# Two more weight units split ahead of the K/V stage, in a pair buffer that stands empty during the first SwiGLU; the attention's output buffer taken at its first use

## The chip, the core and the metric

The kernel runs on one core of a Trainium2 chip. The metric is device time in microseconds (us), the median over runs. TensorE (PE) multiplies matrices, VectorE (DVE), ScalarE (ACT) and GpSimd (POOL) do the elementwise work, and SyncE (SP) issues almost every DMA.

## The reference, cut to what matters

```python
def short_conv_mixer(h, w_in, conv_w, w_out): ...       # layer 0
def swiglu(h, w_gu, w_down):
    g, u = jnp.split(h @ w_gu, 2, axis=-1)
    return (jax.nn.silu(g) * u) @ w_down
...
for layer in range(DEPTH):                               # two layers
    if layer < N_A_LAYERS:
        h = h + short_conv_mixer(rms_norm(h, a_norm[i]), a_w_in[i], a_conv[i], a_w_out[i])
    else:                                                # K/V from the stream after layer 0
        shared = shared_kv(h, kv_norm, w_kv, ...)        # six K/V sets, two of them compressed
        h = h + nsa_mixer(rms_norm(h, b_norm[i]), b_w_qg[i], b_w_o[i], *shared)
    h = h + swiglu(rms_norm(h, f_norm[layer]), f_w_gu[layer], f_w_down[layer])
return rms_norm(h, final_norm)
```

There are 256 tokens, the model is 1024 wide, a SwiGLU is 2816 wide, and everything is float32.

## The kernel before, in words

**Precision by splitting.** Every float32 operand of a matmul is split in two: `hi` is a rounded copy and `lo` is the rest, `x - hi`. A weight unit is a tile of 128 x 1024 that a DMA loads (`w_...`); ACT writes its hi (`h_...`, line 322), and DVE or POOL writes its lo (`l_...`, line 326). A product is then three matmuls (`mm3`, lines 396 to 398: hi by hi, hi by lo, lo by hi), or two in the first 20 of the 22 pieces of a SwiGLU (lines 658 and 660).

**Stages.** Short convolution (from the start to about 105 us), first SwiGLU (to 289 us), K/V and Q projections with the compression MLP (to about 350 us), attention (to 441 us), second SwiGLU, final norm. Between two stages `residual_tail` adds the last products to `h` (DVE, line 523) in four steps, and the next norm's input is formed chunk by chunk, eight chunks in all: `n` hi on ACT (line 447), `n` lo on DVE (line 451), and the square `n_sq` on ACT (line 456). POOL adds the eight squares one after another (`n_acc`, line 461). PE turns the sum (`n_ss`, line 468), DVE and POOL make the reciprocal root from it (`n_ms`, `n_rtok`), PE spreads it (`n_bc`, line 481), and DVE copies it to `n_rbc`; only the gated part of a SwiGLU needs it, the matmuls start before it is there.

**Streams of weights.** `wa` and `wr` are two streams of units. `ahead(n)` loads and splits units until n are ready. The split parts lie in rings of three buffers (tags `a` and `r`); a ring's buffer comes free when PE has read the unit in it. The raw K/V and output units (`w_kv...`, `w_O...`) have four buffers of their own. The K/V units come in the order in which the plan takes them: K2a, K0a, K0b, K1a, K1b, K2b, Q0a, K4a, Q0b, K4b, then the compression weights Y and the values V.

**Large buffers.** `pair` gives 128 x 2 x 2048 floats from three buffers. The inputs of the norms (`n0`, `n1`, and `n2` twice), the compression's input `xc`, every second `pt` and the attention's output `o_all` take turns in them.

**What sets the order.** The program is written once, in order; a scheduler then places each engine's instructions by a timeline of its own, and each engine runs its list strictly in order. `in_order` (table `ord`) names the engines that keep the written order: from the end of the convolution to the second piece of the first SwiGLU these are PE and POOL alone, so there DVE, ACT and SP stand as the scheduler put them. The K/V and attention stage is written by the table `plan`: H is one chunk of the second n2, K, Q, Y, V are matmuls on a unit, A is one unit more of `wa`.

Of the kernel before, what the change touches and what calls it, by code (L numbers as in the profile page):

```python
# [8 lines left out]
F32 = mybir.dt.float32  # L9
# [7 lines left out]
P = 128  # L17
D = 1024
S = 256
KC = D // P  # L20
FH = 2816
NF = FH // P
# [146 lines left out]
 'qdma': 0,  # L169
 'sq': {'n1': 0, 'n3': 1},  # L170
 'units': {'GP': ('a', False),
           'K0a': ('a', False),
           'K0b': ('a', False),
           'K1a': ('r', False),
           'K1b': ('r', False),
           'K2a': ('a', False),
           'K2b': ('a', False),
           'K4a': ('a', False),
           'K4b': ('r', False),
           'O0a': ('r', False),  # L180
# [12 lines left out]
           'O6b': ('a', 'all'),  # L193
           'O7a': ('a', 'both'),
           'O7b': ('r', True),
           'Q0a': ('a', False),
           'Q0b': ('r', False),
           'Q1a': ('a', False),
           'Q1b': ('r', False),
           'Q2a': ('a', False),  # L200
# [13 lines left out]
           'Y12': ('a', False),  # L214
           'Y13': ('r', False)}}
CFG["plan"] = """
H4 K2a H7 K0a A H5 A A K0b A K1a H2 A H0 B0 H1 |4 A K1b H3 NR H6 A A A I NS CR0 CR1 A CB0 K2b Q0a K4a CB1 A
Q0b K4b A Y00 A A A Y10 R0 B1 Y11 A V0 A M0 Y01 A Y02 V1 Y03 J0 Y12 A r A KR4 KR2 A |5 Y13 J1 t0 GP Q1a t1 ck
V2 P0 S0 M1 GR G0 B2 A B3 S1 B4 A C0 S2 V3 G1 B5 N cv A Q1b Q2a r r S3 G2 T0 Q2b R1 D0 P1 R2 S4 G3 A T1 C1 G4
U0 B6 A S5 Q3a C2 G5 B7 T2 S6 W0 D1 T3 Q3b U1 T4 E0 R3 D2 r G6 B8 S7 P2 X0 r T5 G7 W1 U2 C3 B9 O0a T6 E1 W2  # L220
# [7 lines left out]
def trunk(ctx: ExitStack, tc: tile.TileContext, a):  # L228
# [71 lines left out]
    spare = {}  # L300

    def split_weights(src, name, cols, ring, pool):
        if (name[0], ring) in spare:
            w, hi, lo = spare.pop((name[0], ring))
        else:
            if phase["name"] == "attention" or name[0] == "O" or name[:2] == "kv":
                w = wp.tile([P, 1024], F32, tag="raw", name=f"w_{name}", bufs=4)
            else:
                w = phase["pool"].tile([P, 1024], F32, tag="raw", name=f"w_{name}", bufs=12)
            hi, lo = (wp.tile([P, 1024], F32R, tag=ring + hl, name=f"{hl}_{name}", bufs=3) for hl in "hl")  # L310
            if name[0] == "O":
                spare[name[0], ring] = [x[:, cols:] for x in (w, hi, lo)]
            w, hi, lo = (x[:, :cols] for x in (w, hi, lo))
        if isinstance(src, list):
            for r, part in enumerate(src):
                nc.sync.dma_start(out=w[r * DH:(r + 1) * DH], in_=part)
        else:
            nc.sync.dma_start(out=w, in_=src)
        if pool in ("hi", "all"):
            nc.gpsimd.tensor_copy(hi, w)  # L320
        else:
            nc.scalar.activation(hi, w, AF.Copy)  # L322
        cut = {False: 0, True: cols, "both": cols // 2, "hi": 0, "all": cols}[pool]
        for eng, c0, c1 in ((nc.gpsimd, 0, cut), (nc.vector, cut, cols)):
            if c0 < c1:
                eng.tensor_tensor(out=lo[:, c0:c1], in0=w[:, c0:c1], in1=f(hi[:, c0:c1]), op=ALU.subtract)  # L326
        return hi, lo
# [313 lines left out]
    def ffn(layer, norm, last):  # L641
        x = norm.both[0]
        ps, gus, accs, gated = {}, {}, None, []

        def piece(j, p):


            if p == 0:
                ps[j] = [bank(f"pgu{layer}_{j}_{c}") for c in range(2)]
            uh, ul = wa.take()  # L650
            for kk in range(4):
                k = 4 * p + kk
                for c in range(2):
                    cols = slice((2 * kk + c) * P, (2 * kk + c + 1) * P)
                    if j >= NF - 2:
                        mm3(ps[j][c][:, :S], (uh[:, cols], ul[:, cols]), (x[:, 0, k], x[:, 1, k]), k == 0, k == KC - 1)
                        continue
                    nc.tensor.matmul(ps[j][c], uh[:, cols], x[:, :, k], start=k == 0, stop=False,  # L658
                                     skip_group_check=True)
                    nc.tensor.matmul(ps[j][c][:, :S], ul[:, cols], x[:, 0, k], start=False, stop=k == KC - 1,  # L660
                                     skip_group_check=True)
            if p and j < NF - 2:
                gus[j] = both(two(f"gu{layer}_{j}"))
                for c in range(2):
                    nc.scalar.activation(gus[j][:, c], ps[j][c][:, S:], AF.Copy)  # L665
                for c in range(2):
                    nc.vector.tensor_tensor(out=gus[j][:, c], in0=ps[j][c][:, :S], in1=gus[j][:, c], op=ALU.add)  # L667

        def rest(j):
            if j < NF - 2:  # L670
                gu = gus[j]
                nc.gpsimd.tensor_tensor(out=gu, in0=gu, in1=norm.bc.unsqueeze(1).to_broadcast([P, 2, S]), op=ALU.mult)  # L672
            else:
                gu = both(two(f"gu{layer}_{j}"))
                for c in range(2):
                    nc.vector.tensor_tensor(out=gu[:, c], in0=ps[j][c][:, :S], in1=norm.bc, op=ALU.mult)
            sg = one(f"sg{layer}_{j}")
            nc.scalar.activation(sg, gu[:, 0], AF.Silu)  # L678
            av = one(f"av{layer}_{j}")
            nc.vector.tensor_tensor(out=av, in0=sg, in1=gu[:, 1], op=ALU.mult)  # L680
            gated.append(hidden(av, f"a{layer}_{j}"))

        for j in range(NF):
            if j == 2:
                in_order(*ORD[2 if layer == 0 else 7])
            if j == NF - 2 and not last:
                in_order(PE)
            piece(j, 0)
            wa.ahead()
            if j == 1:  # L690
                norm.rstd()
            wr.ahead(min(j + 1, 3))
            piece(j, 1)
            if j == NF - 1:
                rest(j)
            wa.ahead()
            if j == 1:
                norm.spread()
                rest(0)
            if 0 < j < NF - 1:  # L700
                rest(j)
            if j == 1:
                accs = four(f"acc{layer + 1}")
            if last and 3 <= j < 7:
                last(j - 3)
            for i in () if j == NF - 2 else (j - 3, j - 2) if j == NF - 1 else (j - 2,):
                if i < 0:
                    continue
                u = wr.take()
                if not last:  # L710
                    residual_step(accs, u, gated[i], i == 0)
                else:
                    for t in range(2):
                        for c in range(2):
                            by_token(accs, u, gated[i], t, c, i == 0, False)
                if j == NF - 1:
                    wr.ahead()
        return accs, [wr.take(), wr.take()], gated[-2:]
# [240 lines left out]


    probs, cbs, pcs, pts, pos, ofs, outs = {}, {}, {}, {}, {}, {}, {}
    o_all = pair("o_all", [KC, S])

    def scores(n):
        g, j = heads[n]
# [105 lines left out]
        ofs[k] = of  # L1071

    def weighed_split(k):
        x = o_all[:, 0, k], o_all[:, 1, k]
        split(*x, ofs[k], CFG["eng"].get(f"x{k}", "ad"))
        outs[k] = x

# [196 lines left out]
```

## Time and profile before

| what | value |
|---|---|
| median of 3 runs | 642.97 us (642.32 to 643.05) |
| the profiled execution | 642.83 us, of which the span from first to last instruction is 641.0 us |
| PE busy | 619.5 us, 97% of the span |
| DVE busy | 471.2 us, 74% |
| ACT busy | 377.4 us, 59% |
| POOL busy | 279.4 us, 44% |
| granted clock of TensorE, mean | 0.995 of full speed |

A row of a timeline gives start, duration, engine, line, operation, output and inputs, count, and in brackets the idle time before it with what ended it. Rows of one kind that follow each other are merged. On ACT and DVE an instruction starts about 0.1 us before the one ahead of it is recorded as ended. A busy PE is not PE at its peak, since the ends of matmuls are modelled; where it stood still is read from the waits.

### The profile page before, as it was taken

To read this page: it belongs to the slowest core of one execution; us is meant where nothing else is said; L and a number is where in the kernel's file an instruction comes from. 1 tells how busy PE (TensorE), PEld (TensorE's weight loads), DVE (VectorE), ACT (ScalarE), POOL (GpSimd) and SP (SyncE) were. 2 spreads that over 40 slices of the span, in tenths; PEclk is the share of its full clock that TensorE was granted. 3 is DMA by queue.
4 is the path that set the end of the run, shared out by engine and by line. 5 is a ranking of instruction groups with operands and counts; after the bars stand their busy time and mean duration, and the time that the engine had idled before them with its cause. 6 is when DMAs were issued, how large, how long until landed. Compare 5 with 4: busy or idle time off the path is not lost.

```text
span 641.0 us, 11285 instructions
## 1 busy us (share of the span) xinstructions
PE 619.5 (97%) x4158; PEld 568.4 (89%) x4158; DVE 471.2 (74%) x783; ACT 377.4 (59%) x738; POOL 279.4 (44%) x258
## 2 busy tenths in 40 slices
PE   7999999999999999999999999997999999999995
PEld 6999999889999999999989998986888888888894
DVE  5789767866666666679996899787876666666664
ACT  7454447464455555547766988986565555555433
POOL 4054313854443334315100756567754433344423
PEclk9999999999999999999989999999999999999998
DMA  8996672646555554032978410009946655555001
GB/s 289 357 351 216 220 237 94 230 165 201 194 196 183 181 177 152 2 99 68 238 196 258 159 67 2 34 2 361 399 158 198 196 182 182 176 184 165 1 1 66
DMA packets 36360, 109.53 MB, mean 171 GB/s; under 512 B 5713, under 2 KB 8145, under 8 KB 36305
## 3 DMA queue, kind: packets, MB, share of 16 engines
q1 hardware_dynamic: 36160, 108.55, 51.2%
q8 instruction: 33, 0.54, 0.3%
q10 hardware_dynamic: 144, 0.26, 0.1%
q14 instruction: 23, 0.18, 0.1%
HBM read 107.22 MB, written 1.05 MB: 169 GB/s over the span
## 4 chain that ended last, share of the span: by engine, by line
PE 81%; DVE 10%; POOL 4%; issue 2%; DMA 1%; ACT 1%; SPq 0%; POOLq 0%; DVEq 0%; ACTq 0%
PE pgu L658 21%; PE pgu L660 11%; PE acc L397 4%; PE acc L398 4%; PE acc L396 4%; PE acc L726 3%; PE acc L725 3%; PE acc L724 3%; PE pcv L398 2%; DVE n L451 2%; PE pcv L397 2%; PE pcv L396 2%; PE po L1060 1%; POOL l_d L326 1%; PE pgu L398 1%
## 5 line engine op out<-in xcount | busy, mean ns | idle before, releaser
L658 PE MATMUL pgu<-n,h_gu 128*128 128x512 f32 x640 | 226.8, 397 | 2.9 <-DVE n L451 2.8
L660 PE MATMUL pgu<-n,l_gu 128*128 128x256 f32 x640 | 179.3, 281 | 1.1 <-DVE l_gu L326 1.1
L658 PEld LDWEIGHTS pgu<-n,h_gu 128*128 128x128 f32 x640 | 120.1, 188 | 31.0 <-DVE n L451 3.0
L326 DVE TENSOR_TENSOR l_gu<-w_gu,h_gu 128x1024 fp32r<-128x1024 f32 x88 | 117.1, 1332 | 26.6 <-ACT h_gu L322 26.1
L672 POOL TENSOR_TENSOR gu<-gu,n_rbc 128x512 f32<-128x512 f32 x40 | 54.8, 1374 | 166.1 <-DVE gu L667 150.0
L660 PEld LDWEIGHTS pgu<-n,l_gu 128*128 128x128 f32 x640 | 121.0, 189 | 2.3 <-DVE l_gu L326 1.4
L680 DVE TENSOR_TENSOR av<-sg,gu 128x256 f32<-128x256 f32 x44 | 74.4, 1692 | 65.7 <-ACT sg L678 65.5
L326 POOL TENSOR_TENSOR l_d<-w_d,h_d 128x1024 fp32r<-128x1024 f32 x40 | 98.0, 2452 | 4.9 <-ACT h_d L322 4.4
L322 ACT ACTIVATE h_gu<-w_gu 128x1024 fp32r<-128x1024 f32 x88 | 92.6, 1053 | 7.1 <-PE pb L397 3.5
L322 ACT ACTIVATE h_d<-w_d 128x1024 fp32r<-128x1024 f32 x44 | 46.8, 1063 | 27.1 <-PE acc L726 21.2
L418 ACT ACTIVATE a_h<-av 128x256 fp32r<-128x256 f32 x44 | 18.3, 416 | 72.8 <-DVE av L680 72.8
L678 ACT ACTIVATE sg<-gu 128x256 f32<-128x256 f32 x44 | 18.2, 416 | 58.9 <-POOL gu L672 54.2
L397 PE MATMUL acc<-a_l,h_d 128*128 128x256 f32 x176 | 49.5, 282 | 0.3 <-DVE a_l L421 0.3
L396 PE MATMUL acc<-a_h,h_d 128*128 128x256 f32 x176 | 49.3, 282 | 0.5 <-ACT a_h L418 0.5
L398 PE MATMUL acc<-a_h,l_d 128*128 128x256 f32 x176 | 49.3, 281 | 0.0
L326 DVE TENSOR_TENSOR l_in<-w_in,h_in 128x768 fp32r<-128x768 f32 (+1 forms) x33 | 38.8, 1187 | 11.4 <-ACT h_in L322 11.4
L322 ACT ACTIVATE h_in<-w_in 128x768 fp32r<-128x768 f32 (+1 forms) x33 | 27.1, 824 | 30.4 <-PE pb L397 21.8
L398 PE MATMUL pcv<-n,l_in 128*128 128x256 f32 x128 | 36.8, 288 | 1.8 <-DVE l_in L326 1.7
L396 PE MATMUL pcv<-n,h_in 128*128 128x256 f32 x128 | 36.8, 287 | 1.7 <-ACT h_in L322 1.7
L397 PE MATMUL pcv<-n,h_in 128*128 128x256 f32 x128 | 36.4, 284 | 0.0
L665 ACT ACTIVATE gu<-pgu 128x256 f32<-128x256 f32 x80 | 29.6, 370 | 10.9 <-PE pgu L660 10.9
L724 PE MATMUL acc<-h_d,a_h 128*128 128x512 f32 (+1 forms) x88 | 34.8, 395 | 0.0
(428 smaller groups left out, 1666.2 us busy)
## 6 DMA issues: line engine op xcount, KB each, us to landing
w_gu<-in_w_gu SPq DMA_DIRECT2D x88, 512.0 KB, 4.2
w_d<-in_w_down SPq DMA_DIRECT2D x44, 512.0 KB, 3.4
w_in<-in_w_in SPq DMA_DIRECT2D x31, 384.0 KB, 6.4
w_wo<-in_w_out SPq DMA_DIRECT2D x8, 512.0 KB, 6.3
w_kvY<-in_w SPq DMA_DIRECT2D x16, 256.0 KB, 5.1
w_kvV<-in_w_v SPq DMA_DIRECT2D x4, 512.0 KB, 5.9
h<-in_xT SPq DMA_DIRECT2D x3, 256.0 KB, 6.2
out<-y SPq DMA_DIRECT2D x3, 256.0 KB, 2.3
```

What stands on the lines that cost most here:

```text
L322: nc.scalar.activation(hi, w, AF.Copy)
L326: eng.tensor_tensor(out=lo[:, c0:c1], in0=w[:, c0:c1], in1=f(hi[:, c0:c1]), op=ALU.subtract)
L396: nc.tensor.matmul(out, wh, xh, start=start, stop=False, skip_group_check=True)
L397: nc.tensor.matmul(out, wh, xl, start=False, stop=False, skip_group_check=True)
L398: nc.tensor.matmul(out, wl, xh, start=False, stop=stop, skip_group_check=True)
L658: nc.tensor.matmul(ps[j][c], uh[:, cols], x[:, :, k], start=k == 0, stop=False, skip_group_check=True)
L660: nc.tensor.matmul(ps[j][c][:, :S], ul[:, cols], x[:, 0, k], start=False, stop=k == KC - 1, skip_group_check=True)
L665: nc.scalar.activation(gus[j][:, c], ps[j][c][:, S:], AF.Copy)
L672: nc.gpsimd.tensor_tensor(out=gu, in0=gu, in1=norm.bc.unsqueeze(1).to_broadcast([P, 2, S]), op=ALU.mult)
L680: nc.vector.tensor_tensor(out=av, in0=sg, in1=gu[:, 1], op=ALU.mult)
L724: nc.tensor.matmul(out, xh, wh, start=start, stop=False, skip_group_check=True)
L725: nc.tensor.matmul(out, xh, wl, start=False, stop=False, skip_group_check=True)
```

## The change

From the 21st piece of the first SwiGLU on, `ahead` keeps five units ready and not three, so K1a and K1b are split there too. Rings have no room for five; the splits of K2a and K0a go to a pair tile `ahead` (ring `p`). The plan has two A less before K0b and K1a. K1a and K1b go to ring a, K2b and Q0a to ring r, and Q0b to ring a. `o_all` is taken from `pair` where it is first written.

```diff
  'units': {'GP': ('a', False),
-           'K0a': ('a', False),
+           'K0a': ('p', False),
            'K0b': ('a', False),
-           'K1a': ('r', False),
-           'K1b': ('r', False),
-           'K2a': ('a', False),
-           'K2b': ('a', False),
+           'K1a': ('a', False),
+           'K1b': ('a', False),
+           'K2a': ('p', False),
+           'K2b': ('r', False),
...
-           'Q0a': ('a', False),
-           'Q0b': ('r', False),
+           'Q0a': ('r', False),
+           'Q0b': ('a', False),
...
 CFG["plan"] = """
-H4 K2a H7 K0a A H5 A A K0b A K1a H2 A H0 B0 H1 |4 A K1b H3 NR H6 A A A I NS CR0 CR1 A CB0 K2b Q0a K4a CB1 A
+H4 K2a H7 K0a H5 A K0b A K1a H2 A H0 B0 H1 |4 A K1b H3 NR H6 A A A I NS CR0 CR1 A CB0 K2b Q0a K4a CB1 A
...
     def split_weights(src, name, cols, ring, pool):
-        if (name[0], ring) in spare:
+        if ring == "p":
+            if "p" not in spare:
+                ahead = pair("ahead", [2, 1024])
+                spare["p"] = [(ahead[:, u, 0], ahead[:, u, 1]) for u in range(2)]
+            w = wp.tile([P, 1024], F32, tag="raw", name=f"w_{name}", bufs=4)
+            hi, lo = spare["p"].pop(0)
+        elif (name[0], ring) in spare:
...
+        def more(j):
+
+            return 3 if last or j < NF - 2 else 5
+
...
             piece(j, 0)
-            wa.ahead()
+            wa.ahead(more(j))
...
                 rest(j)
-            wa.ahead()
+            wa.ahead(more(j))
...
-    o_all = pair("o_all", [KC, S])
+    o_all = []
...
     def weighed_split(k):
-        x = o_all[:, 0, k], o_all[:, 1, k]
+        if not o_all:
+            o_all.append(pair("o_all", [KC, S]))
+        x = o_all[0][:, 0, k], o_all[0][:, 1, k]
```

Lines of the changed file are 6 to 10 higher than those of the file before (322 is 328, 326 is 332, 451 is 457).

**First place: DVE between the convolution and the first SwiGLU.** `h` is the residual, `n_0_1345` the input of the SwiGLU (`n1`), `l_gu_1_1` and so on the lo parts of SwiGLU weights. Before:

```order
L523 TENSOR_TENSOR h<-acc_2_562,h 128x512
L451 SCALAR_TENSOR_TENSOR n_0_1345<-h,gains,n_0_1345 128x256 x2
L523 TENSOR_TENSOR h<-acc_3_563,h 128x512
L451 SCALAR_TENSOR_TENSOR n_0_1345<-h,gains,n_0_1345 128x256 x6
L326 TENSOR_TENSOR l_gu_1_1_1440<-w_gu_1_1_1438,h_gu_1_1_1439 128x1024
L667 TENSOR_TENSOR gu_0_1466<-pgu_0_0_1420,gu_0_1466 128x256
```

The same place in the changed kernel:

```order
L529 TENSOR_TENSOR h<-acc_2_562,h 128x512
L457 SCALAR_TENSOR_TENSOR n_0_1345<-h,gains,n_0_1345 128x256 x2
L529 TENSOR_TENSOR h<-acc_3_563,h 128x512
L332 TENSOR_TENSOR ahead<-w_kvK2a,ahead 128x1024
L332 TENSOR_TENSOR ahead<-w_kvK0a,ahead 128x1024
L457 SCALAR_TENSOR_TENSOR n_0_1345<-h,gains,n_0_1345 128x256 x6
L332 TENSOR_TENSOR l_gu_1_1_1440<-w_gu_1_1_1438,h_gu_1_1_1439 128x1024
L673 TENSOR_TENSOR gu_0_1466<-pgu_0_0_1420,gu_0_1466 128x256
```

The lo parts of K2a and K0a now stand there, ahead of six of the eight n lo; before, they stood at the end of this SwiGLU. On ACT the two hi parts stand at the same point, behind the first two squares and ahead of the third n hi.

**Second place: PE at the turn of the squares' sum.** `n_acc_1418` is the sum of all eight squares; `pgu_1_0`, `pgu_1_1` are the second piece of the SwiGLU, `pgu_2_1` is of the third. Before:

```order
L660 MATMUL pgu_2_1_1572<-n_0_1345,l_gu_2_0_1473 128x256
L468 MATMUL n_ss<-ident,n_acc_1418 128x128 x2
L658 MATMUL pgu_1_0_1477<-n_0_1345,h_gu_1_1_1439 128x512
L660 MATMUL pgu_1_0_1477<-n_0_1345,l_gu_1_1_1440 128x256
L658 MATMUL pgu_1_1_1478<-n_0_1345,h_gu_1_1_1439 128x512
```

In the changed kernel:

```order
L666 MATMUL pgu_1_1_1478<-n_0_1345,l_gu_1_0_1274 128x256
L474 MATMUL n_ss<-ident,n_acc_1418 128x128 x2
L664 MATMUL pgu_1_0_1477<-n_0_1345,h_gu_1_1_1439 128x512
L666 MATMUL pgu_1_0_1477<-n_0_1345,l_gu_1_1_1440 128x256
L664 MATMUL pgu_1_1_1478<-n_0_1345,h_gu_1_1_1439 128x512
```

The 16 matmuls of the unit gu_2_0, which stood ahead of the turn, now come behind the unit gu_1_1; the turn comes after 48 matmuls of the SwiGLU and not after 64.

**Third place: DVE in the K/V stage, from behind `cf` on.** `cf` is the raw compression input times n_rbc (line 762), `xc` its split form, `l_kvY` and `l_kvV` lo parts of units, `w2s`, `keyf`, `qf` and `q` small steps of this stage. The Y unit that PE takes first after the values is 3899 (lo 3900) in the first list and 3895 (lo 3896) in the second. Before:

```order
L326 TENSOR_TENSOR l_kvY_3719<-w_kvY_3717,h_kvY_3718 128x1024
L778 TENSOR_TENSOR xc<-cf_3738,xc 64x2x240 x4
L778 TENSOR_TENSOR xc<-cf_3740,xc 64x2x240 x4
L326 TENSOR_TENSOR l_kvY_3744<-w_kvY_3742,h_kvY_3743 128x1024
L903 SCALAR_TENSOR_TENSOR qf_3943<-pq_3784,n_rbc 128x512
L326 TENSOR_TENSOR l_kvV_3846<-w_kvV_3844,h_kvV_3845 128x1024
L326 TENSOR_TENSOR l_kvY_3726<-w_kvY_3724,h_kvY_3725 128x1024
L421 TENSOR_TENSOR w2s_3986<-w_0_3983,w2s_3986 128x256
L856 TENSOR_TENSOR keyf_4058<-pkv_3809,n_rbc 128x512
L421 TENSOR_TENSOR q_0_4201<-qf_3943,q_0_4201 64x512
L421 TENSOR_TENSOR q_0_4202<-qf_3943,q_0_4202 64x512
L326 TENSOR_TENSOR l_kvY_3900<-w_kvY_3898,h_kvY_3899 128x1024
```

In the changed kernel:

```order
L332 TENSOR_TENSOR l_kvY_3722<-w_kvY_3720,h_kvY_3721 128x1024
L788 TENSOR_TENSOR xc<-cf_3734,xc 64x2x240 x4
L788 TENSOR_TENSOR xc<-cf_3736,xc 64x2x240 x4
L913 SCALAR_TENSOR_TENSOR qf_3939<-pq_3780,n_rbc 128x512
L332 TENSOR_TENSOR l_kvY_3740<-w_kvY_3738,h_kvY_3739 128x1024
L332 TENSOR_TENSOR l_kvV_3842<-w_kvV_3840,h_kvV_3841 128x1024
L427 TENSOR_TENSOR w2s_3982<-w_0_3979,w2s_3982 128x256
L866 TENSOR_TENSOR keyf_4054<-pkv_3805,n_rbc 128x512
L427 TENSOR_TENSOR q_0_4197<-qf_3939,q_0_4197 64x512
L427 TENSOR_TENSOR q_0_4198<-qf_3939,q_0_4198 64x512
L332 TENSOR_TENSOR l_kvY_3912<-w_kvY_3910,h_kvY_3911 128x1024
L332 TENSOR_TENSOR l_kvY_3896<-w_kvY_3894,h_kvY_3895 128x1024
```

One Y unit (3719 before) is now split ahead of `cf` and so ahead of this list, and the unit 3912 now stands ahead of 3896, where its counterpart stood behind 3900. Both lists have four unit splits and the same small steps from `cf` to the split that ends the list.

## Rows read from the trace of the kernel before

**Rows 1.** The page: span, and busy time of the engines.

```profile
span 641.0 us, 11285 instructions
PE 619.5 (97%) x4158; PEld 568.4 (89%) x4158; DVE 471.2 (74%) x783; ACT 377.4 (59%) x738; POOL 279.4 (44%) x258
```

**Rows 2.** Waits of PE: who waited for whom, total us, times, longest.

```profile
PE pgu L658 <- DVE n L451: 2.8, 3, 1.5
...
PE py L789 <- DVE l_kvY L326: 1.2, 1, 1.2
...
PE acc L396 <- ACT a_h L418: 0.5, 1, 0.5
...
PE acc L397 <- DVE a_l L421: 0.3, 1, 0.3
```

**Rows 3.** One unit's split, K2a, by its tile (duration in ns).

```profile
L322 ACT ACTIVATE h_kvK2a<-w_kvK2a x1: 1047/1047/1047, 276.9 to 276.9; 128x1024 fp32r<-128x1024 f32 x1
L326 DVE TENSOR_TENSOR l_kvK2a<-w_kvK2a,h_kvK2a x1: 1218/1218/1218, 278.8 to 278.8; 128x1024 fp32r<-128x1024 f32 x1
```

**Rows 4.** Timeline of ACT at the start of the first SwiGLU.

```profile
104.80 0.90 ACT L447 ACTIVATE n<-h,gains 128x256 fp32r<-128x256 f32 x2
105.60 1.05 ACT L322 ACTIVATE h_d<-w_d 128x1024 fp32r<-128x1024 f32 x1
...
112.30 0.72 ACT L456 ACTIVATE n_sq<-h 128x256 f32<-128x256 f32 x2
```

**Rows 5.** Timeline of DVE there.

```profile
105.46 0.68 DVE L523 TENSOR_TENSOR h<-acc,h 128x512 f32<-128x512 f32 x1
106.06 0.87 DVE L451 SCALAR_TENSOR_TENSOR n<-h,gains,n 128x256 fp32r<-128x256 f32 x2
...
109.85 1.23 DVE L326 TENSOR_TENSOR l_gu<-w_gu,h_gu 128x1024 fp32r<-128x1024 f32 x1 [0.53 <-ACT h_gu L322]
...
114.96 3.47 DVE L326 TENSOR_TENSOR l_gu<-w_gu,h_gu 128x1024 fp32r<-128x1024 f32 x1 [1.05 <-ACT h_gu L322]
```

**Rows 6.** Timeline of PE there, first matmuls of the SwiGLU.

```profile
105.20 0.50 PE L658 MATMUL pgu<-n,h_gu 128*128 128x512 f32 x1 [0.47 <-DVE n L451]
...
105.67 0.40 PE L658 MATMUL pgu<-n,h_gu 128*128 128x512 f32 x1
...
106.72 0.40 PE L658 MATMUL pgu<-n,h_gu 128*128 128x512 f32 x1
```

**Rows 7.** The sum of squares and its turn, 100 to 120 us, by tile.

```profile
L461 POOL TENSOR_TENSOR n_acc<-n_acc,n_sq x6: 733/829/1413, 107.9 to 114.3; 128x256 f32<-128x256 f32 x6
...
L468 PE MATMUL n_ss<-ident,n_acc x2: 271/272/273, 116.6 to 116.7; 128*128 128x128 f32 x2
```

**Rows 8.** Timeline of POOL there.

```profile
110.27 2.22 POOL L461 TENSOR_TENSOR n_acc<-n_acc,n_sq 128x256 f32<-128x256 f32 x2 [0.35 <-ACT n_sq L456]
112.86 2.15 POOL L461 TENSOR_TENSOR n_acc<-n_acc,n_sq 128x256 f32<-128x256 f32 x2 [0.36 <-ACT n_sq L456]
114.96 2.39 POOL L326 TENSOR_TENSOR l_d<-w_d,h_d 128x1024 fp32r<-128x1024 f32 x1
```

**Rows 9.** Timeline of PE and of DVE in the K/V stage.

```profile
302.10 0.39 PE L398 MATMUL pkv<-n,l_kvK1a 128*128 128x256 f32 x1 [0.26 <-DVE l_kvK1a L326]
...
328.37 0.49 PE L789 MATMUL py<-l_kvY,xc 128*128 128x256 f32 x1 [1.22 <-DVE l_kvY L326]
...
311.65 1.23 DVE L326 TENSOR_TENSOR l_kvK4b<-w_kvK4b,h_kvK4b 128x1024 fp32r<-128x1024 f32 x1 [0.70 <-ACT h_kvK4b L322]
312.80 1.28 DVE L762 TENSOR_TENSOR cf<-pkv,n_rbc 128x512 f32<-128x512 f32 x2
```

**Rows 10.** Windows: stretch, length, busy PE, PEld, DVE, ACT, POOL, granted clock, DMA.

```profile
330.50:333.50 3.00, 3.00 (x15) 3.00 (x14) 2.57 (x4) 2.63 (x4) 0.53 (x1) 0.50 0.94 231
440.00:444.00 4.00, 2.06 (x14) 1.52 (x12) 3.97 (x4) 3.68 (x10) 4.00 (x2) 1.00 1.02 393
...
300.00:430.00 130.00, 126.17 (x926) 119.25 (x924) 114.56 (x351) 104.82 (x280) 55.82 (x103) 0.99 0.41 121
```

## The prediction, made before the changed kernel ran

> **What bounds the kernel now.** The page shows a busy PE for 97% of a span of 641.0 us and DVE, the next engine, for 74% [rows 1]. So the kernel is a string of matmuls, and a change that adds and removes no matmul, as this one, can move the time only by where PE stands still. I read the waits of PE first. From the first SwiGLU on, its longest are those for n lo at the start of a SwiGLU (2.8 us in three waits), one of 1.2 us for a Y unit in the K/V stage, and 0.5 and 0.3 us for the first gated piece of the first SwiGLU [rows 2]. Then I read the timelines of PE and of the engines that it waits for at the three places where the order of instructions moves.
>
> The profiled execution took 642.83 us, 1.83 us more than its span and 0.14 us less than the median of 642.97 us; the sum below starts at 642.83. A shift of under 0.2% (1.3 us) can hardly be told from none here.
>
> **What is removed and added.** The number of unit splits stays as it is. One costs 1.05 us of ACT for hi and 1.22 us of DVE for lo [rows 3]. K1a and K1b leave the K/V stage and take the place that K2a and K0a had at the end of the first SwiGLU; K2a and K0a go to its start. The question is what covers them there. The raw K2a and K0a were loaded in the convolution stage already, so no transfer holds them back. K1a takes the raw buffer that O0a had in that stage (512 KB for twice 256 KB), and K1b and O0a are loaded some 20 us into the SwiGLU, over 140 us before their splits; PE has no wait named for a transfer, and I take these moves as free.
>
> **First term: n lo waits behind two splits.** The third n hi starts on ACT at 104.80, and n lo 3 on DVE at 106.06, when the residual's last step at 105.46 lets DVE go [rows 4, 5]. With the change ACT does the hi of K2a and K0a from 104.80 on, each starting 0.95 after the one ahead (1.05 less the overlap of 0.1), so the third n hi starts at 106.7 and not 104.8. DVE does the lo of K2a at 106.06 (its hi is ready at 105.85) and that of K0a at 107.2, and reaches n lo 3 at 108.3 instead of 106.06, ready 0.47 later at 108.8. PE wants it at 106.72: per chunk of n it does two pairs of a 512- and a 256-wide matmul, and three pairs take 1.05 us, from 105.67 to 106.72 [rows 6]. So PE stands from 106.72 to about 108.87: 2.15 us. The other n lo follow 0.4 us apart, and PE needs 0.7 us for each, so they add nothing. Nothing covers this: PE keeps the written order here, and all its next matmuls need n. The bounds are 1.9 us (the hi and lo overlap better) and 2.9 us (the adds of POOL get between the splits, one of 0.73 us, [rows 7]).
>
> **Second term: the turn of the squares' sum comes earlier on PE, while the sum comes later.** PE turned the sum at 116.6 [rows 7], after 32 pairs; now after 24 pairs, so at 116.6 less 8 times 0.35, 113.8, and with the first term at 115.95. When is the sum ready? Before, POOL's last add ended at 112.86 + 2.15 = 115.0 [rows 8]. The last square ends at 113.0 on ACT [rows 4]; in the changed order the squares 5 to 8 stand together behind a weight's hi, 1.9 us later than before, and again end at 113.0, the first of the four at 112.05. Four adds of 0.73 us each would then end at 115.1, and PE would wait for nothing. But the adds are not alone. DVE's split at 109.85 ended at 111.08; the two adds listed at 110.27 took 2.22 us, as if the first began at 111.08. And the split at 114.96, beside POOL's of 2.39 us from the same moment, took 3.47 us for its usual 1.22 [rows 5, 8]: one waited for the other. In the changed order two splits of DVE, l_gu_1_1 and l_gu_2_0, fall among these four adds, since DVE comes to them 2 to 2.5 us later. In series that is 112.3 + 4 x 0.73 + 2 x 1.15 = 117.5, a stall of 1.55 us; with no split between, 0. I take 1.3, near the upper end, since the rows show the waiting both times.
>
> The Trainium skill, "SBUF — State Buffer", section "SBUF: two separate sides", says that DVE with two inputs in SBUF and a POOL instruction that reads SBUF exclude each other for a whole instruction, whichever starts first. By that rule the second term would be the whole 1.55 us and the sum 0.25 us more; without it, 0. The 3.47 us agree with the rule.
>
> **Third term: the first gated piece.** The chain from the sum over n_rtok and n_rbc to the gated piece made PE wait 0.5 and 0.3 us [rows 2]. The chain is later by about the 2 to 2.5 us of the sum, PE by 3.45 us, but the matmuls that need the piece stand 12 rows further up in its list (some 2 us of work). Between losing these waits (-0.85) and adding as much, I take 0.
>
> **Fourth term: the K/V stage.** The wait for l_kvK1a at 302.10 (0.26 us, [rows 9]) goes, for K1a is ready long before. With the gap behind it PE comes 0.4 us earlier to the Y units. But there it waited till 328.37 for a Y unit's lo [rows 9], and that I follow on DVE. The step cf began at 312.80, behind K4b's lo of 311.65 [rows 9]. K4b is in ring r, and now has to wait for K2b's buffer; PE ends K2b at 310.2, so K4b's hi runs from 310.25 to 311.3, its lo to 312.5, n_rbc's copy follows, and cf begins at 312.85. DVE is one unit ahead there, but from cf to the lo that PE wants four splits and the same small steps stand in both orders: the unit gained goes to the Y unit that now stands ahead of the wanted one. So PE starts again at 328.4 as before, and the 0.4 us gained are lost in a longer wait. I take +0.1 us. The bounds are -1.7 (both waits with the slow restarts gone) and +0.7 (cf later by half a unit, which also holds back xc). The rest of the attention keeps PE's order, and DVE's and ACT's differ by neighbours that change places; I take 0, with 0.7 us to either side.
>
> **Sum.** 2.15 + 1.3 + 0 + 0.1 = 3.55 us: 646.4 us, 0.55% over the time before.
>
> **Rivals.**
> 1. The sum of squares is in time, and the gated piece no longer makes PE wait. 642.83 + 2.15 - 0.85 + 0.1 = 644.2. For it: the last square ends as early as before. Against it: the splits that fall among the adds.
> 2. The K/V stage gives back its waits in full: 646.4 - 1.8 = 644.6. For it: two splits fewer before cf. Against it: K4b's ring and the order behind cf.
> 3. The other side, not slower: DVE bounds the whole stretch from 300 to 430 us, not only at the two waits, and the 2 x 1.15 us of splits that leave it bring its end 2.3 us forward: 646.3 - 2.3 = 644.0, within 0.2%; if rival 1's sum is in time too, 641.8. It decides from a gain of 2.1 us on. For it: DVE is busy for 114.56 of 130 us there. Against it: PE is busy for 126.17 [rows 10], so hardly 4 us are there to be gained at all, and DVE's lead is spent behind cf.
> 4. The two new stalls lower PE's clock. At 330.5 to 333.5 us it was granted half speed, after a stall of 1.2 us [rows 9, 10]. If 3.4 us of the SwiGLU ran so, they would cost 1.7 us: 648.1. Against it: from 440 to 444 PE stood still for nearly half of the time, and the clock stayed full [rows 10].
>
> [...]
>
> **How the numbers follow.** The forecast has a chance of 0.55, with a range of its own from 645.2 to 647.6; rival 1 0.17, rival 2 0.08, rival 3 0.12, rival 4 0.08. The range leaves out the lower part of rivals 1 and 3 and the upper part of rival 4: 643.7 to 648.0. Slower by over 0.2% is above 644.26: the forecast, rival 4, most of rival 2, a third of rival 1, in all 0.75. Within 0.2%: most of rival 1 and half of rival 3, 0.19. Faster: rival 3 with rival 1's sum in time, 0.06.
>
> **What the new profile would show.** First term: PE waits once for n lo, some 2 us, at 107 to 109, and DVE has two `ahead` rows right ahead of that n lo. Second: PE waits 1 to 1.6 us for n_acc at 116 to 118. Third: waits for a_h or a_l near 132 of under 1 us in all. Fourth: no wait for K1a, and one of 1.5 to 1.7 us for a Y unit, PE starting again 3.5 us later than before. The prediction is wrong if n lo makes PE wait for less than 1 us, or if the Y wait is gone and attention begins less than 2 us late.

## The result, and the profile after

The changed kernel takes 646.66 us (median of 6 runs, 646.21 to 647.08), the kernel before 642.85 in the runs beside it: a ratio of 1.0059, 95% interval 1.0046 to 1.0071. The forecast was 646.4. The profiled execution took 647.05 us with a span of 645.3, 4.22 us more than the one of before.

The page of the changed kernel, span and busy time; against [rows 1] PE is busy for 2.5 us more and the span is 4.3 longer:

```profile
span 645.3 us, 11281 instructions
PE 622.0 (96%) x4158; PEld 569.9 (88%) x4158; DVE 473.0 (73%) x783; ACT 378.2 (59%) x738; POOL 277.8 (43%) x258
```

Its waits of PE (who waited for whom, total us, times, longest). Against [rows 2], n lo has gone from 2.8 us to 5.0 (2.0 of it new in the first SwiGLU, 0.2 in the second), n_acc is new, a_h and K1a are gone, the Y unit's wait has grown from 1.2 to 2.1:

```profile
PE pgu L664 <- DVE n L457: 5.0, 4, 2.0
PE py L799 <- DVE l_kvY L332: 2.1, 1, 2.1
...
PE n_ss L474 <- POOL n_acc L467: 1.0, 1, 1.0
...
PE sb L983 <- DVE pt L427: 0.6, 1, 0.6
PE pvc L403 <- DVE w2s L427: 0.4, 1, 0.4
...
PE acc L403 <- DVE a_l L427: 0.2, 1, 0.2
```

The timelines at the start of the first SwiGLU, ACT, DVE, POOL and PE (start, duration; in brackets the idle time before and what ended it):

```profile
104.97 1.05 ACT L328 ACTIVATE ahead<-w_kvK2a 128x1024 fp32r<-128x1024 f32 x1
105.92 1.04 ACT L328 ACTIVATE ahead<-w_kvK0a 128x1024 fp32r<-128x1024 f32 x1
106.86 0.89 ACT L453 ACTIVATE n<-h,gains 128x256 fp32r<-128x256 f32 x2
...
106.22 1.22 DVE L332 TENSOR_TENSOR ahead<-w_kvK2a,ahead 128x1024 fp32r<-128x1024 f32 x1
107.36 1.22 DVE L332 TENSOR_TENSOR ahead<-w_kvK0a,ahead 128x1024 fp32r<-128x1024 f32 x1
108.49 2.95 DVE L457 SCALAR_TENSOR_TENSOR n<-h,gains,n 128x256 fp32r<-128x256 f32 x6
111.90 1.23 DVE L332 TENSOR_TENSOR l_gu<-w_gu,h_gu 128x1024 fp32r<-128x1024 f32 x1 [0.45 <-ACT h_gu L328]
...
114.51 1.23 DVE L332 TENSOR_TENSOR l_gu<-w_gu,h_gu 128x1024 fp32r<-128x1024 f32 x1 [0.53 <-ACT h_gu L328]
...
112.32 1.41 POOL L467 TENSOR_TENSOR n_acc<-n_acc,n_sq 128x256 f32<-128x256 f32 x1 [0.27 <-ACT n_sq L462]
...
114.62 1.71 POOL L467 TENSOR_TENSOR n_acc<-n_acc,n_sq 128x256 f32<-128x256 f32 x1
...
109.03 0.50 PE L664 MATMUL pgu<-n,h_gu 128*128 128x512 f32 x1 [2.00 <-DVE n L457]
...
117.20 0.44 PE L474 MATMUL n_ss<-ident,n_acc 128*128 128x128 f32 x2 [0.97 <-POOL n_acc L467]
```

The reader sees the two early splits ahead of the third n hi and the third n lo, and the stall of 2.00 us that follows. Of the last four adds of the squares, the first and the third take 1.41 and 1.71 us, and the other two 0.74 and 0.73. Each long one has a split of DVE beside it and ends 0.6 us behind the end of that split (113.13 and 115.74). In all the four take 4.83 us, up to the turn. In the kernel before two of the last four were long too (1.41 and 1.32 us), but the first of the four began 2.05 us earlier, at 110.27.

Where the time went, read off the timelines of PE in both profiles (start of the stage's first matmul, or end of its last):

| point on PE | before | after | later by |
|---|---|---|---|
| first matmul of the first SwiGLU | 105.20 | 105.37 | 0.17 |
| first matmul of K0b (stage K/V) | 298.34 | 301.12 | 2.78 |
| end of K4b | 322.49 | 324.76 | 2.27 |
| first attention score | 353.26 | 356.33 | 3.07 |
| last matmul of O7b (end of attention) | 441.12 | 445.27 | 4.15 |
| last matmul | 633.67 | 637.97 | 4.30 |

So the SwiGLU costs 2.6 us, the units up to K4b give 0.5 back, the Y units take 0.8, the attention takes 1.1, the rest 0.15; 0.17 stand ahead of the SwiGLU.

### The profile page after: what moved, and what is told of

It is laid out like the page before. It is cut to its first block, busy times and chain, and to the rows that moved or that the text cites. A ratio compares the mean times of both kernels' runs of the same rounds, so it can differ in the third digit from the quotient of the medians.

```text
span 645.3 us, 11281 instructions
## 1 busy us (share of the span) xinstructions
PE 622.0 (96%) x4158; PEld 569.9 (88%) x4158; DVE 473.0 (73%) x783; ACT 378.2 (59%) x738; POOL 277.8 (43%) x258
## 4 chain that ended last, share of the span: by engine, by line
PE 80%; DVE 9%; ACT 3%; POOL 2%; DMA 2%; issue 2%; SPq 1%; POOLq 0%; DVEq 0%; ACTq 0%
PE pgu L664 21%; PE pgu L666 11%; PE acc L403 4%; PE acc L402 4%; PE acc L404 4%; PE acc L736 3%; PE acc L735 3%; PE acc L734 3%; PE pcv L404 2%; PE pcv L402 2%; PE pcv L403 2%; DVE p L992 1%; DMA w_kvK1a<-in_w_kv 1%; PE po L1070 1%; POOL l_d L332 1%
## 5 line engine op out<-in xcount | busy, mean ns | idle before, releaser
L332 DVE TENSOR_TENSOR l_gu<-w_gu,h_gu 128x1024 fp32r<-128x1024 f32 x88 | 113.7, 1293 | 24.2 <-ACT h_gu L328 23.2
```

## Experiments

Each change of time below is the ratio to the kernel before, run beside it on the same chip. For the stages of a run I give what it loses against the kernel before between the points of the table, from its own profile: SwiGLU, units up to K4b, from there to the first score (the Y units), attention, rest. A profile is of one execution, which can lie off the median of its run: by 0.9 us under it in early_only, 0.55 under it in early_pool, 1.7 under it in late_pool and 2.1 over it in spread.

**The lazy buffer alone.** The kernel before with the edit of `o_all` only.

```diff
-    o_all = pair("o_all", [KC, S])
+    o_all = []
```

> The kernel before, with only the output buffer of the attention taken at its first use. The order on every engine is that of before. Theory A: nothing waits for that buffer, 642.6 us, within 0.2% of before. Theory B: the buffer that it now gets comes free later or collides with another use, some tenths of a us to 1 us more, between 360 and 390 us.

Measured: 642.49 us, 1.0003 (0.9995 to 1.0012). This part of the change costs nothing that the runs can tell from zero. One thing in its profile limits how finely single profiles may be read: with the order of before, its wait for the Y unit was 1.92 us and not 1.22. PE ended K4b 1.83 us earlier than in the profile of before, but K4b's hi on ACT had to wait for its transfer till 309.44 (310.56 in the other), only 1.12 earlier:

```profile
309.44 1.06 ACT L322 ACTIVATE h_kvK4b<-w_kvK4b 128x1024 fp32r<-128x1024 f32 x1 [2.17 <-DMA w_kvK4b<-in_w_kv]
...
327.25 0.49 PE L789 MATMUL py<-l_kvY,xc 128*128 128x256 f32 x1 [1.92 <-DVE l_kvY L326]
```

**The early splits alone.** The kernel before with the new branch of `split_weights` and two lines of the table.

```diff
-           'K0a': ('a', False),
+           'K0a': ('p', False),
-           'K2a': ('a', False),
+           'K2a': ('p', False),
```

> The kernel before, with nothing changed but that the splits of K2a and K0a go to the pair tile (so they stand at the start of the first SwiGLU); rings, plan and the number of units kept ready are those of before. Theory A: PE waits once for n lo near 109 (2.0 us) and once for n_acc near 117 (1.0), the first gated piece waits less (-0.65), and the K/V stage keeps its waits for K1a (0.3) and for a Y unit (1.2): 642.85 + 2.4 = 645.2 us. Theory B, the loss of the whole change comes from rings and order in the K/V stage and the attention, which are as before here: 642.9 us.

Measured: 645.52 us, 1.0046 (1.0030 to 1.0063), as theory A says. Stages: 2.7, 0.0, -0.3, -0.2, -0.15. Both stalls are there, with the rings and the plan of before:

```profile
108.61 0.50 PE L664 MATMUL pgu<-n,h_gu 128*128 128x512 f32 x1 [1.98 <-DVE n L457]
...
116.85 0.33 PE L474 MATMUL n_ss<-ident,n_acc 128*128 128x128 f32 x1 [0.92 <-POOL n_acc L467]
```

**The same splits later.** The changed kernel, with the raw K2a and K0a in the ring of twelve raw buffers that the SwiGLU's weights use, so that they are loaded, and split, at the 18th piece.

```diff
-            w = wp.tile([P, 1024], F32, tag="raw", name=f"w_{name}", bufs=4)
+            w = phase["pool"].tile([P, 1024], F32, tag="raw", name=f"w_{name}", bufs=12)
             hi, lo = spare["p"].pop(0)
```

> Theory A, by the terms of the prediction: the early splits alone cost the stalls at the start of the first SwiGLU. In this kernel they stand at its 18th piece, so PE's wait for n lo at 109.03 (2.00 us) and the one for n_acc at 117.20 (0.98) are gone, and the waits of before for the first gated piece (0.51 and 0.35) come back in place of 0.2: 2.0 + 1.0 - 0.65 = 2.35 us less, 644.3 us, with the Y unit's wait in the K/V stage still some 2 us. Theory B, the K/V stage is held by DVE and takes up what the SwiGLU loses: PE comes 2.4 us earlier to the Y unit and waits that much longer there, 646.6 us as the changed kernel. Theory C, moving the two splits out of the K/V stage does bring DVE's end there forward once nothing is lost before: 642 us or less.

Measured: 644.52 us, 1.0030 (1.0017 to 1.0043). Stages: 1.0, -0.5, 0.8, 0.0, 0.5. B and C fall. The time is near theory A's, but only in part by its way: the SwiGLU gives back 1.6 us of the 2.35, and the attention, of which the theory says nothing, another 1.1. The stalls at 107 to 117 are gone, but the SwiGLU still loses 1.0 us, since DVE now does both lo in one piece, and the unit's lo that PE wants stands behind them (rows of DVE and PE):

```profile
251.26 2.32 DVE L332 TENSOR_TENSOR ahead<-w_kvK2a,ahead 128x1024 fp32r<-128x1024 f32 x1 [2.56 <-ACT ahead L328]
253.84 1.21 DVE L332 TENSOR_TENSOR ahead<-w_kvK0a,ahead 128x1024 fp32r<-128x1024 f32 x1
254.97 1.21 DVE L332 TENSOR_TENSOR l_gu<-w_gu,h_gu 128x1024 fp32r<-128x1024 f32 x1
...
256.24 0.38 PE L666 MATMUL pgu<-n,l_gu 128*128 128x256 f32 x1 [0.33 <-DVE l_gu L332]
...
329.62 0.50 PE L799 MATMUL py<-l_kvY,xc 128*128 128x256 f32 x1 [2.06 <-DVE l_kvY L332]
```

The wait for the Y unit is 2.06 us, as in the changed kernel, though PE comes 1.9 us earlier to it.

**The turn where it stood.** The changed kernel, with the units of the first SwiGLU taken in the order gu_1_0, gu_2_0, gu_1_1, so that the turn of the sum comes after 64 matmuls again.

```diff
+        if layer == 0:
+            units[3], units[4] = units[4], units[3]
...
             if j == 1:
+                if layer == 0:
+                    piece(2, 0)
+                    wa.ahead(more(j))
                 norm.rstd()
```

> The changed kernel, with the turn of the squares' sum put back on PE behind the unit gu_2_0, ahead of gu_1_1, as it stood in the kernel before; the early splits stay. Theory A: the 2.0 us for n lo stay, the 0.98 for n_acc go, since 5.6 us of matmuls now stand ahead of the turn; the gated piece comes no earlier, and its matmuls wait for at most 0.5 us more: 0.5 to 1 us less than the changed kernel, 645.7 to 646.2. Theory B, what PE does not wait for n_acc it waits for the gated piece, whose chain starts at the same sum: 646.7, no change.

> The run late_turn a second time, for a second profile. In the first one PE's clock was granted at half from 108.3 to 111.5 us, right behind the 2 us wait for n lo, and some 1 us went there; in the changed kernel, early_only and k4b_ring the same wait left it full. Theory A, the clock is a matter of the single execution: here it is full at 108 to 112, the first SwiGLU ends 1.2 us later than before (from the SwiGLU's own start) and not 2.2. Theory B, it goes with this order of work: half again at that place.

Measured: 646.41 us, 1.0060 (1.0038 to 1.0083), and the second time 645.36, 1.0051 (1.0036 to 1.0065). Stages: 2.2, -0.5, 0.9, 0.75, 1.2, and 2.05, -0.5, 0.9, 0.9, 0.4. The wait for n_acc is gone both times, so it is the place of the turn that made it. But only 0.4 to 0.55 us of its 1.0 are gained in the SwiGLU, between the two theories, and by the times alone the gain can't be told from nothing. In the second profile the gated piece waits again as before [rows 2], 0.91 us in all against 0.16 in the changed kernel:

```profile
131.41 0.62 PE L405 MATMUL acc<-a_h,h_d 128*128 128x256 f32 x3 [0.56 <-ACT a_h L427]
132.38 0.39 PE L406 MATMUL acc<-a_l,h_d 128*128 128x256 f32 x1 [0.35 <-DVE a_l L430]
```

In the first profile the gated piece does not wait, and the time went to the clock, which was granted at half behind the 2 us stall (0.50, the lower of its two levels, 1.2 and 2.4 GHz); in the second one it was full there. Windows, first run and then second (stretch, length, busy PE, PEld, DVE, ACT, POOL, granted clock, DMA):

```profile
109.00:110.00 1.00, 1.00 (x5) 0.85 (x4) 1.00 (x2) 0.73 (x3) 0.70 (x2) 0.50 0.85 268
110.00:111.00 1.00, 1.00 (x5) 0.81 (x5) 0.18 (x1) 1.00 (x2) 0.78 (x1) 0.50 0.66 250
```

```profile
108.00:112.00 4.00, 4.00 (x25) 3.52 (x24) 3.19 (x5) 3.94 (x11) 2.93 (x3) 1.00 0.62 198
```

**K4b's ring.** The changed kernel, early splits and all, with two rings exchanged.

```diff
-           'K4b': ('r', False),
+           'K4b': ('a', False),
-           'Y00': ('a', False),
+           'Y00': ('r', False),
```

> The changed kernel, with the rings of K4b and of the first Y unit exchanged: K4b (ring a now) waits for K1b's buffer and not for K2b's, 3 us less, and in the order that this gives DVE does the Y unit that PE wants ahead of the other one. Theory A, the fourth term: cf begins about 1 us earlier than at 315.78, the wanted lo is ready about 1.1 us earlier again, and PE's wait of 2.08 us for it falls to 0 to 0.3: 1.8 to 2 us less, 644.7 to 644.9 us. Theory B, DVE's load bounds the whole stretch: the wait goes here and comes back at the next units, 646.5. Theory C, the load of the first Y unit, for which ACT waited till 311.96, holds cf: cf stays at 315.8, only the exchange of the two Y units counts, 645.6.

Measured: 644.37 us, 1.0030 (1.0019 to 1.0041). Stages: 2.6, -0.5, -0.3, -0.1, -0.1. That is 0.3 to 0.5 us under theory A's time, and not by its way; B and C fall by the time. PE came to this stage 0.7 us earlier than in the profile of the changed kernel; cf began at 314.92 where it began at 315.78, so by PE's clock only some 0.2 earlier, not 1. K4b's lo comes early (310.24), but now the first Y unit, in ring r, waits for K2b's buffer, and DVE does it ahead of cf. So the exchange moves the wait for that buffer to another unit ahead of cf and does not take it away:

```profile
310.24 1.23 DVE L332 TENSOR_TENSOR l_kvK4b<-w_kvK4b,h_kvK4b 128x1024 fp32r<-128x1024 f32 x1
313.33 1.23 DVE L332 TENSOR_TENSOR l_kvY<-w_kvY,h_kvY 128x1024 fp32r<-128x1024 f32 x1 [1.86 <-ACT h_kvY L328]
...
314.92 1.29 DVE L772 TENSOR_TENSOR cf<-pkv,n_rbc 128x512 f32<-128x512 f32 x2
...
329.68 0.49 PE L799 MATMUL py<-l_kvY,xc 128*128 128x256 f32 x1 [0.69 <-DVE l_kvY L332]
```

What counts there is the order of the two Y units behind cf, which has turned: the wanted lo comes first, and the wait falls by 1.4 us, the stage by 1.1. Another 1.1 us come from the attention, where DVE's order is again that of the kernel before.

**The early lo on POOL.** The changed kernel with K2a and K0a marked True in the table, so that POOL does their lo.

```diff
-           'K0a': ('p', False),
+           'K0a': ('p', True),
...
-           'K2a': ('p', False),
+           'K2a': ('p', True),
```

> The changed kernel with the two early splits where they are, but their lo on POOL: DVE's list at the start of the first SwiGLU is that of before, ACT still does the two hi first, and POOL does the two lo ahead of six of the seven adds of the squares. Theory A, as in the prediction's first term both engines hold n lo back, ACT by 1.9 us and DVE by another 1: n hi 3 starts at 106.86 as in the changed kernel, its lo is ready at 107.9 and not at 109.0, so PE waits 0.9 to 1.1 us in place of 2.0; the adds end about 116 to 117, PE comes to the turn at about 115, and its wait for n_acc is 1 to 2 us: 645.6 to 646.6 in all. Theory B, DVE alone is what holds n lo: no wait at 107, one of 1 to 2 us for n_acc, 645 or less. Theory C, ACT alone: the wait stays at 2.0, 646.7 or more.

Measured: 649.69 us, 1.0118 (1.0103 to 1.0133). Stages: 6.45, -0.5, 0.9, 0.8, -0.25. A and B fall; C has the wait and the time by its numbers, but not its reason, for ACT's n hi holds DVE back by 1.08 us only. The wait for n lo stays at 1.95 us, and another of 1.40 follows, though DVE has no early split left. DVE, POOL and PE, and a window behind the stalls (columns as in [rows 10]):

```profile
106.15 6.11 DVE L457 SCALAR_TENSOR_TENSOR n<-h,gains,n 128x256 fp32r<-128x256 f32 x6 [1.08 <-ACT n L453]
...
105.04 2.36 POOL L332 TENSOR_TENSOR ahead<-w_kvK2a,ahead 128x1024 fp32r<-128x1024 f32 x1
107.37 2.55 POOL L332 TENSOR_TENSOR ahead<-w_kvK0a,ahead 128x1024 fp32r<-128x1024 f32 x1
...
107.74 0.50 PE L664 MATMUL pgu<-n,h_gu 128*128 128x512 f32 x1 [1.95 <-DVE n L457]
110.25 0.79 PE L664 MATMUL pgu<-n,h_gu 128*128 128x512 f32 x1 [1.40 <-DVE n L457]
...
112.00:115.00 3.00, 3.00 (x11) 2.52 (x11) 1.48 (x2) 1.45 (x3) 1.64 (x2) 0.50 0.17 65
```

The six n lo take 6.11 us and not 2.95. Taken singly, the first three take 1.53, 2.59 and 0.95 us and end 0.28 us behind the end of the instruction that POOL has running (its two subtractions and an add), and the other three take 0.47 to 0.48. So work on POOL is no cover for DVE here. Not all of the 6.45 us is due to that: from 108.4 to 115.2 us the clock was granted at half, where a pair of matmuls took 0.64 us and not 0.35; over the eight pairs from 110.25 on that is some 2.3 us.

**Ways to a cheaper place.** late_pool is late_load with the lo on POOL; spread is the changed kernel with one split at about the 7th piece and one at about the 13th; the runs with _ring add the exchange of k4b_ring.

```diff
+            if not last and j in (9, 15):
+                u = "K2a" if j == 9 else "K0a"
+                done["kv" + u] = split_weights(takes[u][0], "kv" + u, takes[u][1], *CFG["units"][u])
             piece(j, 1)
```

> The run late_load (the two early splits moved to the 18th piece of the first SwiGLU), with their lo parts on POOL and not on DVE. In late_load PE waited there twice for a unit's lo from DVE (0.33 and 0.23 us, 0.9 with the slow restarts). Theory A: DVE came late since it had the two lo, 2.3 us, to do; on POOL they cost nothing, and the time is 0.9 us under late_load: 643.6 us. Theory B: it is the two hi on ACT, 2 us, that held back the units' hi and so their lo: the waits stay, 644.5.

> late_pool, and the rings of K4b and the first Y unit exchanged as in k4b_ring. Theory A, the terms add: nothing lost in the first SwiGLU, 0.5 us gained at K1a, and from there to the end of the K/V stage the 0.3 us that k4b_ring gained against the kernel before: 0.8 us less than the kernel before, 641.8 us. Theory B, k4b_ring gained only because PE came 2 us late into the K/V stage, which gave DVE and the loads that much time: without that loss the wait for the Y unit is back to 1.2 us or more, 642.6 or above.

> The changed kernel, with the splits of K2a and K0a moved apart: one at about the 7th piece of the first SwiGLU, one at about the 13th. In late_load, with both in one piece, PE waited there for a unit's lo, 0.9 us with the slow restarts. Theory A: DVE has room for one split in a piece (it is busy for 96 of 143 us there), so nothing is lost in the SwiGLU against the kernel before; then 0.5 us gained at K1a and 0.8 lost at the Y unit: 642.6 + 0.3 = 642.9 us. Theory B: a split of 1.2 us more makes a unit's lo late in any piece, since each lo waits for its hi and has no lead; 0.4 us for each: 643.7.

> spread, and the rings of K4b and the first Y unit exchanged as in k4b_ring. Theory A, the terms add: no loss in the SwiGLU, and from there to the end of the K/V stage the 0.8 us less that k4b_ring showed: 641.8 us, under the kernel before. Theory B, the gain of k4b_ring needs PE to come late: 642.6 or more.

| run | us | profiled execution | ratio | SwiGLU | to K4b | Y units | attention | rest |
|---|---|---|---|---|---|---|---|---|
| late_pool | 646.63 | 644.90 | 1.0059 (1.0043 to 1.0075) | 1.7 | -0.5 | 0.9 | 0.0 | 0.1 |
| late_pool_ring | 644.94 | 644.86 | 1.0038 (1.0023 to 1.0052) | 2.9 | -0.5 | -0.1 | 0.2 | 0.7 |
| spread | 643.99 | 646.09 | 1.0027 (1.0014 to 1.0039) | 2.2 | -0.5 | 1.0 | 0.5 | 0.0 |
| spread_ring | 643.92 | 643.92 | 1.0018 (1.0004 to 1.0032) | 1.9 | -0.5 | -0.3 | 0.0 | 0.4 |

Theory A's time falls in all four. B's is near in spread only. In late_pool the time lies above both theories; in the two runs with the exchange it lies above 642.6, as B has it, but not for B's reason, since the wait for the Y unit was 0.67 and 0.69 us. The terms of the K/V stage add as expected: with the exchange the Y units cost nothing or gain 0.3, without it they lose 0.8 to 1.0, wherever the splits stand. But no place tried in the SwiGLU was free. On POOL the lo took 2.58 and 3.39 us in late_pool (2.57 and 2.38 in late_pool_ring), and PE waited up to 0.90 us (2.10) for a unit's lo from DVE. In spread and spread_ring the first split made PE wait for nothing; the second one stood on ACT for its transfer (as the first had, without harm), and the units behind it came late. The listed wait is the smaller part of that: some 1.0 us more is lost in both runs up to 268 us, in steps of 0.1 to 0.2 us that are too short to be listed as waits (rows of ACT and PE, spread_ring):

```profile
210.47 1.06 ACT L328 ACTIVATE ahead<-w_kvK0a 128x1024 fp32r<-128x1024 f32 x1 [1.69 <-DMA w_kvK0a<-in_w_kv]
...
214.32 0.39 PE L669 MATMUL pgu<-n,l_gu 128*128 128x256 f32 x1 [0.47 <-DVE l_gu L332]
```

No version that moves the two splits beats the kernel before; spread_ring comes nearest, 0.18% behind.

## Why the prediction was right

**First term, n lo behind two splits: 2.15 us said, a wait of 2.00 measured** (counted from the start of the SwiGLU, the matmul behind it starts 2.14 us later than before). The mechanism is shown by the runs: early_only has it with nothing else changed, late_load loses it when the splits go elsewhere. The instants came out as worked out, shifted by the 0.17 us of the start: n hi 3 at 106.86 (106.7), the lo of K0a at 107.36 (107.2), n lo 3 at 108.49 (108.3).

**Second term, the turn: 1.3 said, 0.97 measured.** That the turn's earlier place makes the wait is shown by late_turn. Why the adds were slow is as argued: two splits of DVE fall among the four, and the add beside each ends 0.6 us behind it. The first of these splits had begun 0.4 us ahead of its add, so the two cost 1.7 us together and not the 2.3 of the series. What I did not price is that this term and the third share a chain. In late_turn_again the turn does not wait and the gated piece does, 0.56 and 0.35 us, so the term is worth about half of its wait.

**Third term, the gated piece: 0 said.** The waits of 0.51 and 0.35 [rows 2] shrank to one of 0.16, so PE waits for 0.7 us less, inside the bounds of -0.85 to +0.85. Listed waits of the SwiGLU sum to 2.00 + 0.97 + 0.16 - 0.86 = 2.27; the measured 2.6 holds 0.3 more. A listed wait is shorter than the delay that it makes (2.00 against 2.14 at the first), since it counts from the end of the matmul ahead, and matmuls overlap.

**Fourth term, the K/V stage: +0.1 said, +0.3 measured** (-0.5 to K4b, +0.8 at the Y units). K1a's wait went, and the Y unit's wait was longer, 2.08 us where 1.5 to 1.7 were said. The steps that I followed are there (ACT and DVE):

```profile
311.96 1.06 ACT L328 ACTIVATE h_kvY<-w_kvY 128x1024 fp32r<-128x1024 f32 x1 [3.93 <-DMA w_kvY<-in_w]
312.94 1.06 ACT L328 ACTIVATE h_kvK4b<-w_kvK4b 128x1024 fp32r<-128x1024 f32 x1
...
315.78 1.29 DVE L772 TENSOR_TENSOR cf<-pkv,n_rbc 128x512 f32<-128x512 f32 x2
...
329.10 2.36 DVE L332 TENSOR_TENSOR l_kvY<-w_kvY,h_kvY 128x1024 fp32r<-128x1024 f32 x2
```

K4b's hi runs when PE is done with K2b. Against PE's end of K4b, cf came 0.7 us later than before, where the prediction had some 0.45. Whether K2b's buffer sets cf, as the prediction has it, stays open: ACT is done at the same moment with the first Y unit, whose transfer it awaited till 311.96, and in k4b_ring the first Y unit waits for that buffer in K4b's place; cf began 2.8 us behind the hi of the unit that waits in the changed kernel and 2.7 in k4b_ring. What was right is the last step, that the unit ahead of the wanted one takes the time that DVE has gained; with these two exchanged the wait was 0.67 to 0.69 us in three runs. A single profile can move this stage by 0.8 us: with the order of before it cost 0.8 in lazy_only and -0.3 in early_only. That all seven profiles with the changed kernel's order have 0.8 to 1.0, and the three with the exchange -0.3 to -0.1, shows that the order counts; the size of the term against the kernel before is known to some 0.5 us only.

**The term taken as nothing: attention, 0 said with 0.7 to either side, 1.1 measured.** The size was beyond the bound, and the reason given was wrong for DVE, whose order was said to differ by neighbours that change places. The attention starts 3.07 us later, but w2s lo stands 6.23 us later on DVE, and PE waits for it; near 382 us it waits for pt and pc too (DVE before, then DVE and PE after):

```profile
356.26 0.41 DVE L421 TENSOR_TENSOR w2s<-w,w2s 128x256 fp32r<-128x256 f32 x1
...
362.49 0.41 DVE L427 TENSOR_TENSOR w2s<-w,w2s 128x256 fp32r<-128x256 f32 x1
...
362.96 0.24 PE L403 MATMUL pvc<-w2s,hv 128*64 128x64 f32 x1 [0.43 <-DVE w2s L427]
...
382.42 0.30 PE L983 MATMUL sb<-kh,q 128*128 128x128 f32 x1 [0.60 <-DVE pt L427]
```

By the tiles' names, PE's order in the attention is the same in all thirteen profiles, as predicted. DVE's order comes in two forms: that of the changed kernel in four of them (the changed kernel, both of late_turn, early_pool), whose attention cost 0.75 to 1.1 us, and that of the kernel before in the other nine, where it cost 0.5 or less. The waits of 0.43 and 0.60 us are in those four and in no other. PE falls back by 0.6 us at w2s and by 0.45 around 382 us, which is the 1.1. So the cost belongs to DVE's order; why the scheduler chose it is not shown.

The sum was near partly by luck, because errors cancel: 3.45 us said for the SwiGLU and 2.6 measured, 0.1 from there to the end of the attention and 1.4 measured.

**The rivals.** Rival 1 falls: the sum was not in time. Rival 2 falls: the K/V stage gave nothing back. Rival 3, DVE as the bound, falls by late_load and spread: with two splits fewer in the K/V stage and no stall at the start of the SwiGLU, the stretch from K0b to the end of the attention took 0.3 and 1.0 us more than before, and not 2.3 less. Rival 4, the clock, is half true. In the changed kernel the clock stayed full through the two stalls of the first SwiGLU, as it did in early_only, k4b_ring and late_turn_again; in late_turn and early_pool it fell to half behind the first of them. In the second SwiGLU of the changed kernel it was low behind the n lo waits, where it was full before (windows of the changed kernel and of before):

```profile
448.00:452.00 4.00, 3.21 (x11) 2.54 (x12) 4.00 (x8) 2.79 (x6) 2.57 (x4) 0.69 1.03 412
```

```profile
444.00:448.00 4.00, 3.04 (x13) 2.00 (x13) 4.00 (x8) 2.99 (x5) 2.56 (x4) 1.00 1.03 415
```

The stages from there on took only 0.15 us more all the same, and a wait of before is gone there, which the prediction's list of the longest waits leaves out:

```profile
448.62 0.39 PE L660 MATMUL pgu<-n,l_gu 128*128 128x256 f32 x1 [1.13 <-DVE l_gu L326]
```

The two go together: the six profiles with the full clock there have this wait, 1.12 to 1.14 us, and the seven with a stretch at half clock wait for 0.25 us or less.

The Trainium skill, "SBUF — State Buffer", section "SBUF: two separate sides", has DVE with two inputs and POOL exclude each other. Two runs bear that out: in early_pool the three slow n lo end 0.28 us behind POOL's instruction, and in the changed kernel the two slow adds end 0.6 us behind DVE's split.

## What to carry to other kernels

That a buffer is empty does not make the work that fills it free: where instructions are placed as soon as their inputs are there, work whose data lies ready can land at the start of the next stage, where each engine is needed for the chain that starts that stage. Ask of moved work when its engine has a lead there, and whether its transfer has landed by then; another engine is no cover where its work slows the first one. And a unit taken out of a busy stage gives time only if what stands next in line is what the bound waits for.

## What the runs showed of the hardware that was not expected

- Beside POOL's subtractions of 2.36 and 2.55 us, six instructions of DVE took 6.11 us and not 2.95; beside DVE's splits of 1.23 us, two adds of POOL took 1.41 and 1.71 us and not 0.73. The one held back ended 0.28 us (DVE) or 0.6 us (POOL) behind the other, and its wait shows as a longer instruction, not as idle time.
- The same program, with the same stall of 2 us, was granted half the clock behind it in one execution (0.50 from 109 to 111 us) and the full one in another. The loss did not add: with the slow clock PE no longer waited at 131 us, and the SwiGLU took 2.2 us more than before in the one and 2.05 in the other.
- Half the clock need not cost time. Behind the wait for the Y unit the kernel before ran at 0.50 [rows 10] and early_only at 1.00, and in either the matmuls on Y units started every 0.22 to 0.23 us, 15 of them in the window of 3 us. In early_pool, on the pairs of the SwiGLU, it cost 0.29 us a pair. The window of early_only:

```profile
332.60:335.60 3.00, 3.00 (x15) 2.99 (x14) 2.56 (x4) 2.73 (x4) 0.53 (x1) 1.00 0.97 253
```

- In the kernel before with only the lazy buffer, whose time is the same, the wait for a Y unit was 1.92 us and not 1.22: waits of a stage that loads hold move by 0.7 us between profiles.
